# Rotary embedding on one core: VectorE's first product of its own row moved to the head of its own tile, and the last tile stored in one transfer

## The chip, the cores and the metric

One core of a Trainium2 chip runs the kernel. The metric is device time in microseconds (us), each kernel measured in repeated runs beside the kernel before on the same chip. "Span" is the time from the first to the last instruction of one profiled execution, some 1.8 us less than the device time of the same run.

## The reference, cut to what matters

```python
batch, seq, dim = (16, 512, 1024)          # float32, 16 heads of 64
x1, x2 = (x[..., :half_dim], x[..., half_dim:])
rotated = concatenate([x1 * cos - x2 * sin, x1 * sin + x2 * cos], axis=-1)
```

It reads 33.5 MB and writes 33.5 MB. Each output is two products and a sum: the element times its cosine, plus its partner in the other half of the head times plus or minus the sine.

## The kernel before: the parts that the change touches

The work goes in 8 tiles of 128 partitions and 8 rows (4 MB each), with room for five tiles at once. In each tile VectorE multiplies by the cosine into PSUM, GpSimd makes the sine products of rows 1 to 7, and VectorE adds two rows at a time (three pairs). Row 0, "its own row", has both products made by VectorE, and row 3 has its sine product from GpSimd. For these two rows TensorE adds the sine product to the cosine product in one PSUM accumulator, `own_ps`, and ScalarE copies the sum out. Row 0 and row 3 take turns in that accumulator.

```python
    def own_row(t):
        r0 = rows(t, ROW_OWN)
        own_product(t, r0)                 # in place, after cos_product has read r0
        ...                                # TensorE adds swapped(r0) to own_ps
        nc.scalar.copy(out=r0, in_=own_ps)

    cos_product(own_ps, 0, ROW_OWN)
    for t in range(NT):
        b1 = sin_rows(t, first[0], 2)
        if t > 0:
            own_row(t)
        p1 = pair_product(t, first[0])
        ...
        pair_sum(*p1, b1)
        p2 = pair_product(t, second[0])
        cos_product(own_ps, t, ROW_PE)     # row 3
        ...
        nc.scalar.copy(out=rows(t, ROW_PE), in_=own_ps)
        ...
        pair_sum(*p2, b2)
        p1 = pair_product(t, third[0])
        if t + 1 < NT:
            cos_product(own_ps, t + 1, ROW_OWN)
        pair_sum(*p1, b1)
        stores(t)                          # last tile: 4 rows, then 4 rows
```

All loads and stores of tiles are issued by SyncE.

## Time and profile before

| | before |
|---|---|
| device time, median of 6 runs | 163.12 us (163.02 to 163.49) |
| span of the profiled run | 161.1 us (its device time: 162.85) |
| busy: VectorE, GpSimd, TensorE, ScalarE | 85%, 79%, 40%, 11% |
| main DMA queue, share of sixteen engines | 97.4% |

How to read it: the prediction below shows the lines. A DMA share is a mean over sixteen engines. A stretch with share 1.00 has all of them at work. The packets of one transfer are dealt out to all sixteen. In short stretches a packet is counted where it starts, so in quarters of a microsecond a share can exceed 1, and 131 GB/s is one packet of 32 KB (131 GB/s x 0.25 us), 66 GB/s one of 16 KB, 82 GB/s one of 20 KB.

### The profile page before, as it was taken

Reading aid. Unit: us, or ns where it says so; the run is one execution under the profiler, and the core shown is the slowest. Engines: PE = TensorE matmul, PEld = TensorE weight load, DVE = VectorE, ACT = ScalarE, POOL = GpSimd, SP = SyncE. Lnnn points to the kernel's source line nnn. Section 1 sums busy time; section 2 is a strip of 40 time slices with the busy share of each in tenths; the row PEclk is TensorE's granted clock in tenths of the full one; section 3 lists DMA queues with packets and bytes.
Section 4 is the critical chain, followed back from the end, with each engine's and each line's share of the span. In section 5 each row is a group of like instructions: output and inputs, shape, how many; then the busy total and the mean of one; then the engine's idle time right before and its main releaser. Section 6 shows DMA issues by size and latency. Waiting matters only on the chain.

```text
span 161.1 us, 432 instructions
## 1 busy us (share of the span) xinstructions
PE 63.7 (40%) x72; PEld 20.4 (13%) x72; DVE 137.1 (85%) x77; ACT 18.5 (11%) x20; POOL 126.9 (79%) x38
## 2 busy tenths in 40 slices
PE   2363480535317170717144450808062622626000
PEld 0122020202011110202020200202020201111000
DVE  1159999999899999999899989999899989999400
ACT  3010201020202020020202020010102020202000
POOL 1195999999499999999999599972999999960000
PEclk9999959555855855595558555555955585557755
DMA  5999999799699699699999999698999999998994
GB/s 181 405 422 457 415 496 521 309 472 521 285 472 545 260 521 521 260 456 456 391 441 464 399 521 505 277 521 382 391 415 496 391 415 488 399 415 374 387 456 199
DMA packets 2257, 67.25 MB, mean 418 GB/s; under 512 B 272, under 2 KB 272, under 8 KB 336
## 3 DMA queue, kind: packets, MB, share of 16 engines
q1 hardware_dynamic: 2208, 67.18, 97.4%
q10 hardware_dynamic: 48, 0.07, 0.1%
q14 instruction: 1, 0.01, 0.0%
HBM read 33.69 MB, written 33.55 MB: 417 GB/s over the span
## 4 chain that ended last, share of the span: by engine, by line
DVE 46%; DMA 25%; PE 12%; issue 6%; ACT 3%; SPq 1%; DVEq 0%; ACTq 0%
DMA xt<-in_x_dram 25%; DVE xt L202 20%; DVE pd L153 18%; PE own_ps L187 12%; DVE xt L159 4%; DVE own_ps L153 4%; ACT xt L232 3%; SPq L78 1%; SPq L88 0%; DVEq L202 0%; ACTq L232 0%; DVEq L159 0%; DVEq L153 0%
## 5 line engine op out<-in xcount | busy, mean ns | idle before, releaser
L176 POOL TENSOR_TENSOR b<-xt,sns 128x2048 f32<-128x2048 f32 (+1 forms) x32 | 126.1, 3979 | 15.9 <-DMA xt<-in_x_dram 15.9
L202 DVE TENSOR_TENSOR xt<-pd,b 128x2048 f32<-128x2048 f32 x24 | 54.9, 2287 | 1.1 <-POOL b L176 0.2
L153 DVE TENSOR_TENSOR pd<-xt,cos_t 128x2048 f32<-128x2048 f32 x24 | 55.0, 2294 | 0.5
L187 PE MATMUL own_ps<-xt,ident 128*128 128x512 f32 x32 | 29.2, 1067 | 44.8 <-DVE xt L159 29.4
L187 PE MATMUL own_ps<-b,ident 128*128 128x512 f32 x32 | 29.3, 1072 | 33.3 <-DVE own_ps L153 30.9
L153 DVE TENSOR_TENSOR own_ps<-xt,cos_t 128x1024 f32<-128x1024 f32 x16 | 19.6, 1226 | 5.9 <-PE cos_t L123 2.8
L187 PEld LDWEIGHTS own_ps<-xt,ident 128*128 128x128 f32 x32 | 9.4, 324 | 64.5 <-issue 64.5
L187 PEld LDWEIGHTS own_ps<-b,ident 128*128 128x128 f32 x32 | 9.2, 316 | 52.9 <-issue 35.2
L194 ACT COPY xt<-own_ps 128x1024 f32<-128x1024 f32 x8 | 8.1, 1012 | 66.1 <-PE own_ps L187 66.1
L232 ACT COPY xt<-own_ps 128x1024 f32<-128x1024 f32 x8 | 8.1, 1012 | 54.8 <-PE own_ps L187 54.8
L159 DVE TENSOR_TENSOR xt<-xt,small 128x1024 f32<-128x1024 f32 x8 | 9.7, 1210 | 0.0
L124 DVE TENSOR_SCALAR sns<-small 128x256 f32<-128x256 f32 x1 | 0.4, 424 | 4.5 <-PE small L117 4.5
L117 PE MATMUL small<-sin_sb,spread 32*128 32x256 f32 x4 | 2.2, 661 | 2.7 <-DMA sin_sb<-in_sin_dram 2.7
L123 PE MATMUL cos_t<-cos_sb,spread 32*128 32x512 f32 x2 | 2.1, 1136 | 1.8 <-DMA cos_sb<-in_cos_dram 1.8
L117 PEld LDWEIGHTS small<-sin_sb,spread 32*128 32x128 f32 x4 | 1.2, 318 | 4.6 <-issue 4.6
L100 PE MATMUL own_ps<-zero 128*128 128x512 bf16 x2 | 1.0, 620 | 1.2 <-DVE zero L97 1.2
L125 ACT ACT_TABLE_LOAD x1 | 1.3, 1283 | 1.2 <-PEq L258 1.2
L97 DVE MEMSET zero<- 128x256 uint32 x1 | 0.3, 272 | 0.9 <-PEq L258 0.9
L125 ACT COPY sns<-small 128x256 f32<-128x256 f32 x1 | 0.4, 372 | 4.1 <-DVE sns L124 4.1
L128 ACT ACTIVATE sns<-small 128x256 f32<-128x256 f32 x1 | 0.4, 386 | 3.9 <-PE small L117 3.9
L120 DVE COPY small<-sns 128x64 f32<-128x64 f32 x2 | 0.4, 224 | 0.4 <-ACT sns L125 0.4
L123 PEld LDWEIGHTS cos_t<-cos_sb,spread 32*128 32x128 f32 x2 | 0.5, 308 | 2.5 <-DMA cos_sb<-in_cos_dram 2.5
(9 smaller groups left out, 1.6 us busy)
## 6 DMA issues: line engine op xcount, KB each, us to landing
out_dram<-xt SPq DMA_DIRECT2D x5, 4096.0 KB, 23.9
xt<-in_x_dram SPq DMA_DIRECT2D x3, 4096.0 KB, 21.4
out_dram<-xt SPq DMA_DIRECT2D x2, 2048.0 KB, 8.1
xt<-in_x_dram SPq DMA_DIRECT2D x1, 2560.0 KB, 12.1
xt<-in_x_dram SPq DMA_DIRECT2D x1, 1536.0 KB, 6.7
sin_sb<-in_sin_dram ACTq DMA_DIRECT2D x1, 64.0 KB, 4.0
cos_sb<-in_cos_dram SPq DMA_DIRECT2D x1, 64.0 KB, 6.7
xt<-in_x_dram SPq DMA_DIRECT2D x2, 34.8
```

Source lines behind the costliest of these rows:

```text
L78: nc.sync.dma_start(out=place, in_=x_v[at])
L100: nc.tensor.matmul(out=ps, lhsT=zero[:, :P], rhs=zero, start=True, stop=True)
L117: nc.tensor.matmul(out=sin_t, lhsT=spread, rhs=part, start=True, stop=True)
L123: nc.tensor.matmul(out=cos_t, lhsT=spread, rhs=cos_sb, start=True, stop=True)
L125: nc.scalar.copy(out=sns[:, :KK, 1, :], in_=sin_k)
L153: nc.vector.tensor_tensor(out=o, in0=i, in1=cb, op=ALU.mult)
L159: nc.vector.tensor_tensor(out=heads(r), in0=heads(r), in1=s, op=ALU.mult)
L176: nc.gpsimd.tensor_tensor(out=o, in0=i, in1=sb, op=ALU.mult)
L187: nc.tensor.matmul(out=ps, lhsT=ident, rhs=other, start=False, stop=True, skip_group_check=True)
L194: nc.scalar.copy(out=r0, in_=own_ps)
L202: nc.vector.tensor_tensor(out=r, in0=ps, in1=b, op=ALU.add)
L232: nc.scalar.copy(out=rows(t, ROW_PE), in_=own_ps)
```

## The change

Its intent: VectorE waited 0.5 us a tile for ScalarE to free the accumulator; with the last pair sum put ahead of the next tile's own-row product, the wait should be covered. And one store in place of two saves an issue and sends larger packets.

```diff
-        elif t == NT - 1:
-            store(t, 0, LAST_OUT)
-            store(t, LAST_OUT, KK)
         elif t > 1:
             store(t)
...
-    cos_product(own_ps, 0, ROW_OWN)
     for t in range(NT):
         first, second, third = PAIRS
         b1 = sin_rows(t, first[0], 2)
+        cos_product(own_ps, t, ROW_OWN)
         if t > 0:
             own_row(t)
...
         p1 = pair_product(t, third[0])
-        if t + 1 < NT:
-            cos_product(own_ps, t + 1, ROW_OWN)
         pair_sum(*p1, b1)
         stores(t)
```

More of the change, by code (lines that the diff above doesn't have):

```diff
@@ L23 @@
 FIRST = 3
-LAST_OUT = 4
 @with_exitstack
```

## The prediction

> **What bounds the kernel now.** I read the page's rows over time and its queue table first, then the stretches (windows), then VectorE's order of time, then SyncE's. From the page, the DMA row in 40 slices and the main queue:
>
> ```profile
> DMA  5999999799699699699999999698999999998994
> q1 hardware_dynamic: 2208, 67.18, 97.4%
> ```
>
> The main queue's packets fill 97.4% of sixteen engines' span, while VectorE has 85% and GpSimd 79%. The stretches show that this is a rate limit with one hole in it (columns: stretch, its length, busy time and count of PE, PEld, DVE, ACT, POOL, the granted clock, DMA share, GB/s):
>
> ```profile
> 2.00:148.00 146.00, 62.85 (x71) 20.24 (x70) 134.05 (x74) 17.10 (x20) 126.15 (x32) 0.65 1.00 431
> 148.00:149.50 1.50, 0.00 (x0) 0.00 (x0) 1.40 (x2) 0.56 (x1) 0.00 (x0) 1.00 0.29 120
> 149.50:159.20 9.70, 0.00 (x0) 0.00 (x0) 1.14 (x1) 0.00 (x0) 0.00 (x0) 0.56 0.98 416
> ```
>
> From 2 to 148 us the share is 1.00 at 431 GB/s: loads, then loads and stores, always queued. At 148 the queue runs dry: every earlier store has gone and the last tile isn't ready. Then the last tile's 4 MB take the final 9.7 us alone. SyncE's order of time shows what ends the hole:
>
> ```profile
> 134.59 0.33 SPq L82 DMA_DIRECT2D out_dram<-xt  x1
> 148.59 0.33 SPq L82 DMA_DIRECT2D out_dram<-xt  x1
> 150.67 0.33 SPq L82 DMA_DIRECT2D out_dram<-xt  x1
> ```
>
> The first is tile 6's whole store, the others the two halves of tile 7's. The first half goes at 148.59, as soon as ScalarE's copy of row 3 ends (147.55 + 1.01 = 148.56). It needs neither of the last VectorE sums. The second follows the last sum (148.35 + 2.29 = 150.64) and queues behind the first, so its time hides. The end of the span therefore hangs on the first byte of tile 7's store, plus 9.7 us of transfer, plus completion.
>
> The inferred chain puts 46% on VectorE, which is true of what delays that first byte, but not of the 146 us before. One VectorE period, tile 5's head to tile 6's head:
>
> ```profile
> 95.83 1.23 DVE L153 TENSOR_TENSOR own_ps<-xt,cos_t 128x1024 f32<-128x1024 f32 x1 [0.50 <-ACT xt L232]
> 96.96 2.29 DVE L202 TENSOR_TENSOR xt<-pd,b 128x2048 f32<-128x2048 f32 x1
> 99.16 1.21 DVE L159 TENSOR_TENSOR xt<-xt,small 128x1024 f32<-128x1024 f32 x1
> 100.29 2.29 DVE L153 TENSOR_TENSOR pd<-xt,cos_t 128x2048 f32<-128x2048 f32 x1
> 102.69 2.29 DVE L202 TENSOR_TENSOR xt<-pd,b 128x2048 f32<-128x2048 f32 x1
> 105.01 2.30 DVE L153 TENSOR_TENSOR pd<-xt,cos_t 128x2048 f32<-128x2048 f32 x1
> 107.22 1.22 DVE L153 TENSOR_TENSOR own_ps<-xt,cos_t 128x1024 f32<-128x1024 f32 x1
> 108.35 2.28 DVE L202 TENSOR_TENSOR xt<-pd,b 128x2048 f32<-128x2048 f32 x1
> 110.67 2.30 DVE L153 TENSOR_TENSOR pd<-xt,cos_t 128x2048 f32<-128x2048 f32 x1
> 113.47 1.23 DVE L153 TENSOR_TENSOR own_ps<-xt,cos_t 128x1024 f32<-128x1024 f32 x1 [0.50 <-ACT xt L232]
> ```
>
> The period is 113.47 - 95.83 = 17.64 us. The only wait in it is 0.50 us, the own-row product waiting for ScalarE to free the accumulator (own_ps). The reader should also take three kinds of start-to-start distance from these rows. An instruction after an independent one starts early: 1.13 after a one-row product, 2.20 to 2.21 after a two-row one. A product that reuses the accumulator just read by the sum in front of it starts 2.32 after. A sum straight after the product that it reads starts 2.40 after (100.29 to 102.69). So order alone costs up to 0.2 us a place.
>
> **What the Trainium skill says.** "DMA: Bandwidth & Descriptors", Specifications, gives a fabric ceiling of 435 GB/s and a first-byte latency of about 0.6 us for transfers issued from sync. The 431 GB/s above agree with the first, so faster compute can't shorten those 146 us; in quarter-microsecond stretches the burst after the issue at 148.59 appears at 149.25 to 149.50, so some 0.7 to 0.9 us here. "Perfetto Trace Analysis", DMA Optimizations, says that splitting a transfer may let some of it start sooner, where the DMA engines are idle; they are, at 148 to 149.5, and the first half is out 2.08 us before the second. "VectorE: DVE Perf Modes", The TRN2 errata, has (N+151)/0.96 ns for an fp32 tensor_tensor: 2291 ns for 2048 elements, where the rows have 2280 to 2300. The same page, The DRAIN you can't avoid, says a semaphore between neighbours costs nothing extra. These rows differ: 2.40 with the dependence against 2.21 without.
>
> **The change, part by part.**
>
> First part, the order on VectorE. No instruction is added or removed on any compute engine. In the new order the last sum follows its own product directly, and the own-row product is followed directly by the in-place product of the same row. That one overwrites what the own-row product has just read, and its semaphore is now one of a direct neighbour. A new period, from start to start:
> - own-row product to in-place product: 1.23 plus the gap of about 0.11 seen after a product written to PSUM (2.40 - 2.29) = 1.34. No row of before has this pair; 1.13 if it isn't held.
> - in-place product to first pair product 1.13; to its sum 2.40; to the second product 2.32; to the row-3 product 2.21; to the second sum 1.13; to the third product 2.32: together 11.51.
> - third product to the last sum 2.40 (2.21 + 0.59, the wait with its gap, before).
> - last sum to the next own-row product 2.20.
> Sum 17.45, against 17.64. The 0.5 us wait goes entirely: ScalarE's copy ends 2.8 us after the third product starts, and the own-row product now comes 4.6 after. But about 0.3 of it comes back as two dependences between neighbours, and 0.19 a period is left.
>
> Tile 0 to 1 had no wait (third product 23.00, own-row product 25.21), so there the new order only costs: the first pair product of tile 1 goes from 29.67 to about 30.07. From there one period brings tile 2's to 47.52 (47.38 before, after a 0.58 wait for its load, landed at 42.82, which the later place no longer meets). Five more periods: 47.52 + 5 x 17.45 = 134.77, against 135.57. Tile 7's remaining work is the same 15.07 us (135.57 to 150.64). VectorE ends at 149.84, 0.8 us earlier.
>
> Second part, one store. It waits for the last sum: issue at 149.84 + 0.03 = 149.87, in place of 148.59. The first byte comes 1.28 us later. Earlier stores are issued one or two microseconds sooner, but they join a queue that is full anyway, and the queue still runs dry at about 148. On the other side, the packets are of 32 KB and not 16 KB. An estimate from the rates above (9.7 us at 416 GB/s against 431 in the long stretch, where packets are of 32 KB and more) is at most 0.3 us; I take 0.13 off for it. One issue of 0.33 us less was hidden.
>
> Net: 0 over the streaming part, +1.28 - 0.13 = +1.15 at the end. The unprofiled time of 163.12 becomes about 164.2 (164.27, pulled down a little for a smaller neighbour gap).
>
> **Rivals.**
> - *The wait goes and the time with it.* Seven places of 0.5 us would be 3.5 us, some 159.6 us, faster by over 2%. For it: the chain has 46% VectorE and shows the ScalarE copy in it. Against: 431 GB/s for 146 us; VectorE's gain can only reach the hole at 148, which is about 1 us.
> - *The last store is hidden.* If VectorE got to the end by 148 or sooner, the queue would never dry and the kernel would gain that 1 us: about 162.2. That needs 0.45 us saved in each of six periods; the dependences take most of that.
> - *VectorE gains nothing.* If the neighbour gaps eat the whole 0.5 us, the store issues at 150.67, 2.08 us later: 163.12 + 2.08 - 0.13 = 165.1.
> - *No neighbour gap at the in-place product* (1.13, not 1.34). Seven places give 1.5 us back, VectorE ends at 148.4, the store issues 0.2 us before the first half did, and with the packets' 0.13 the time is 162.8.
> - *GpSimd becomes the bound.* Its products for a tile take 3 x 4.52 + 2.35 = 15.9 us, under 17.45, and they end at 143.4. Its waits are for loads, which don't move. I give it little.
>
> **Range and chances.** 164.2 us, with 163.3 to 164.9 eight times in ten: the low end is most of the way to the unheld in-place product, the high end near the rival without gain. The three timed runs of before lie within 0.36 us. Two per cent is 3.26 us either way. Nothing above reaches 166.4; 159.9 needs the transfer limit to be wrong. Faster 0.01, within 2% 0.97, slower 0.02.
>
> **What would show it.** In the changed profile: no ScalarE wait ahead of the own-row product; last sums 2.40 after their product; in-place products 1.34 after the own-row product; a period of 17.45; DMA share 1.00 until about 148, then a hole longer by a good microsecond; a single issue near 149.9; some 9.6 us of transfer after it. I am wrong if the hole is gone, if the streaming part itself gets faster or slower than 431 GB/s, or if the in-place pair has another distance, which moves the end by 0.07 us for each 0.01.

## The result, and the profile after

The changed kernel took 163.44 us (median of 6 runs, 163.18 to 163.76) against 163.12. The ratio is 1.0015, with a 95% interval of 0.9999 to 1.0031. A ratio here is the mean time of one kernel's fast runs over that of the other's of the same rounds, so it isn't quite the ratio of the medians. It is 0.24 us of 163.2, where 1.1 was forecast. The time lies in the predicted range, but the difference is less than a quarter of the one forecast, and not clear of noise.

The page's DMA row and main queue, the stretches, and SyncE's last issue (same columns as in the prediction):

```profile
DMA  5999999699699799799999999898999999996996
q1 hardware_dynamic: 2064, 67.18, 97.0%
```

```profile
2.00:148.00 146.00, 63.73 (x71) 20.41 (x70) 135.49 (x75) 17.66 (x20) 126.17 (x32) 0.68 1.00 430
148.00:149.50 1.50, 0.00 (x0) 0.00 (x0) 1.50 (x1) 0.00 (x0) 0.00 (x0) 1.00 0.11 44
149.50:159.20 9.70, 0.00 (x0) 0.00 (x0) 0.30 (x1) 0.00 (x0) 0.00 (x0) 0.51 0.88 378
```

```profile
149.87 0.33 SPq L81 DMA_DIRECT2D out_dram<-xt  x1
```

The streaming part is as it was (1.00, 430 GB/s), the hole is longer, and the single store issues at 149.87 us, which is the predicted figure. VectorE's order of time, one period from tile 5's head to tile 6's:

```profile
97.59 1.22 DVE L152 TENSOR_TENSOR own_ps<-xt,cos_t 128x1024 f32<-128x1024 f32 x1
98.84 1.22 DVE L158 TENSOR_TENSOR xt<-xt,small 128x1024 f32<-128x1024 f32 x1
99.98 2.29 DVE L152 TENSOR_TENSOR pd<-xt,cos_t 128x2048 f32<-128x2048 f32 x1
...
110.36 2.29 DVE L152 TENSOR_TENSOR pd<-xt,cos_t 128x2048 f32<-128x2048 f32 x1
112.75 2.29 DVE L201 TENSOR_TENSOR xt<-pd,b 128x2048 f32<-128x2048 f32 x1
114.96 1.22 DVE L152 TENSOR_TENSOR own_ps<-xt,cos_t 128x1024 f32<-128x1024 f32 x1
...
147.50 2.29 DVE L201 TENSOR_TENSOR xt<-pd,b 128x2048 f32<-128x2048 f32 x1
```

From tile 1 on no wait is left. (One of 0.40 us for ScalarE stands in tile 0, at 19.90; the first profile of before has none there, the second has the same.) The period is 114.96 - 97.59 = 17.37 us (17.64 before, 17.45 predicted). The in-place product comes 1.25 after the own-row product, the last sum 2.39 after its product. So VectorE did what was forecast; it ended at 149.79 us, forecast 149.84. What was wrong comes after that.

The end in quarters of a microsecond shows it. Before:

```profile
148.75:149.00 0.25, 0.00 (x0) 0.00 (x0) 0.25 (x1) 0.00 (x0) 0.00 (x0) 1.00 0.31 131
149.00:149.25 0.25, 0.00 (x0) 0.00 (x0) 0.25 (x1) 0.00 (x0) 0.00 (x0) 1.00 0.00 0
149.25:149.50 0.25, 0.00 (x0) 0.00 (x0) 0.25 (x1) 0.00 (x0) 0.00 (x0) 1.00 1.38 590
...
158.50:158.75 0.25, 0.00 (x0) 0.00 (x0) 0.00 (x0) 0.00 (x0) 0.00 (x0) 0.50 2.16 918
158.75:159.00 0.25, 0.00 (x0) 0.00 (x0) 0.00 (x0) 0.00 (x0) 0.00 (x0) 0.50 0.31 131
159.00:159.25 0.25, 0.00 (x0) 0.00 (x0) 0.00 (x0) 0.00 (x0) 0.00 (x0) 0.50 0.15 66
```

After:

```profile
148.75:149.00 0.25, 0.00 (x0) 0.00 (x0) 0.25 (x1) 0.00 (x0) 0.00 (x0) 1.00 0.31 131
149.00:149.25 0.25, 0.00 (x0) 0.00 (x0) 0.25 (x1) 0.00 (x0) 0.00 (x0) 1.00 0.01 0
...
159.00:159.25 0.25, 0.00 (x0) 0.00 (x0) 0.00 (x0) 0.00 (x0) 0.00 (x0) 0.50 1.22 524
159.25:159.50 0.25, 0.00 (x0) 0.00 (x0) 0.00 (x0) 0.00 (x0) 0.00 (x0) 0.50 3.66 1573
```

In both, a single 32 KB packet of tile 6 starts as late as 148.75 to 149.00 us. At 1.21 us for such a packet, the engine that carries it is busy until about 150.1. In before, the other fifteen begin tile 7 from 149.25 on, and that one engine only when it is done; at the end it is alone with the last 16 KB packet (66 GB/s in 159.00 to 159.25). It had no hole, and it set the end. In the changed kernel all engines are idle when the store's first bytes come (150.70 in the packet records; the late engine is done at 150.10). They start together and finish together: the last packets of four start at 159.00 to 159.25 and those of twelve at 159.25 to 159.50, with no straggler.

The packet records (every packet's start, length, queue and size, kept with each trace) give the sizes, counted here from the span's start. They carry no engine number; the ends of the sixteen engines are those of the last sixteen packets that close the store. The fifteenth ends at 159.43 before and at 160.60 after: 1.17 us later, where 1.15 was predicted. But the end of before is the sixteenth engine's, at 159.86, and that of after is at 160.61, so the end moved by 0.75 only (the spans by 0.72). The first profile of before is also a run on the fast side, 162.85 us for a median of 163.12. A second pair of profiles, told below, has a smaller step still.

### The profile page after: what moved, and what is told of

It reads as the page before. It is cut to its first block, busy times and chain, and to the rows that moved or that the text cites. A ratio compares the mean times of both kernels' runs of the same rounds, so it can differ in the third digit from the quotient of the medians.

```text
span 161.8 us, 432 instructions
## 1 busy us (share of the span) xinstructions
PE 64.5 (40%) x72; PEld 20.5 (13%) x72; DVE 137.8 (85%) x77; ACT 18.5 (11%) x20; POOL 126.9 (78%) x38
## 4 chain that ended last, share of the span: by engine, by line
DVE 35%; DMA 33%; POOL 13%; issue 9%; PE 2%; ACT 1%; DVEq 0%; POOLq 0%; SPq 0%
DMA xt<-in_x_dram 17%; DMA out_dram<-xt 17%; DVE pd L152 15%; DVE xt L201 14%; POOL b L175 13%; DVE own_ps L152 2%; PE own_ps L186 2%; DVE xt L158 2%; ACT xt L193 1%; DVE small L119 0%; DVEq L201 0%; POOLq L175 0%; SPq L77 0%; SPq L81 0%
## 5 line engine op out<-in xcount | busy, mean ns | idle before, releaser
L186 PE MATMUL own_ps<-xt,ident 128*128 128x512 f32 x32 | 29.7, 1081 | 42.7 <-DVE xt L158 22.2
```

What stands on the lines that cost most here:

```text
L186: nc.tensor.matmul(out=ps, lhsT=ident, rhs=other, start=False, stop=True, skip_group_check=True)
```

## The experiments

Two theories were put to the chip. **A**: one DMA engine runs about a packet behind the others and sets the end; the hole is free until that engine is done. **B**, the prediction's: each microsecond by which the first byte comes later counts in full. "3+5" and "4+4" are the rows in the last tile's two stores.

| run | order | last store | issue of tile 7's first byte | median us | ratio to before | 95% | fifteen engines end, the last ends |
|---|---|---|---|---|---|---|---|
| before_again | old | 4+4 | 148.75 | 163.24 | 1.0002 | 0.9977 to 1.0027 | 159.57, 160.34 |
| after_again | new | one | 149.56 | 163.44 | 1.0017 | 0.9994 to 1.0040 | 160.29, 160.46 |
| store_only | old | one | 150.83 | 164.55 | 1.0086 | 1.0065 to 1.0108 | 161.55, 161.58 |
| order_only | new | 4+4 | 147.64 | 163.26 | 1.0014 | 0.9995 to 1.0033 | 159.04, 160.14 |
| split3 | old | 3+5 | about 140.9 | 163.17 | 1.0013 | 0.9992 to 1.0034 | 158.87, 160.07 |
| order_split3 | new | 3+5 | about 139.7 | 163.03 | 1.0005 | 0.9984 to 1.0026 | 159.02, 160.56 |
| after_cos_first | new | one | 149.14 | 163.42 | 1.0030 | 1.0004 to 1.0055 | 159.88, 160.66 |
| after_late | new | one | 152.10 | 165.65 | 1.0163 | 1.0137 to 1.0189 | 162.81, 162.84 |

(The two "about" figures come from rows in which the view merges two issues: the row's end less one issue of 0.33 us. The last column is from the packet records of the profiled run; the first profiles have 159.43, 159.86 before and 160.60, 160.61 after. The runs were made in several sessions, each beside the kernel before on its own chip; issues and ends are those of one profiled run, the ratios those of four to six runs.)

The last column shows A at a glance. Where the hole is closed (order_only, split3, order_split3), fifteen engines end some 0.4 to 0.7 us earlier than in the two profiles of before, and the last ends at 160.07 to 160.56, where those two have 159.86 and 160.34.

### store_only: the second part alone

```diff
-        elif t == NT - 1:
-            store(t, 0, LAST_OUT)
-            store(t, LAST_OUT, KK)
```

> The order of before, with the last tile's store in one transfer: the second part of the change alone. The store must wait for the last sum, so it should issue near 150.7 us where the first half issued at 148.6 before, and all sixteen DMA engines stand idle for about 2 us. Theory A (one DMA engine runs about one packet behind the others, is still busy with tile 6 when the first half issues, and sets the end of before; for the other fifteen the hole is free up to about half a microsecond): 2.08 us later first byte, less 0.44 us that the laggard had cost at the end, less 0.1 us for larger packets: +1.3 to +1.5 us, about 164.5 us. Theory B (the prediction: every microsecond of later first byte counts in full): +1.95 us, about 165.1 us.

Measured 164.55 us, +1.40 by the ratio. SyncE's order of time has the issue at 150.83, 2.24 us later than before:

```profile
150.83 0.33 SPq L82 DMA_DIRECT2D out_dram<-xt  x1
```

A's figure, not B's: the interval is 1.06 to 1.76, and B has 1.95. Some 0.8 us of the delay was free, what larger packets save included.

### order_only: the first part alone

```diff
+LAST_OUT = 4
...
+        elif t == NT - 1:
+            store(t, 0, LAST_OUT)
+            store(t, LAST_OUT, KK)          # the rest as in the changed kernel
```

> The new order on VectorE, with the last tile's store still in two halves: the first part of the change alone. The first half should issue 0.7 us earlier than before (near 147.8). Theory A (one DMA engine behind the others sets the end): the first byte for fifteen engines comes earlier, the laggard's does not, the time is that of before within 0.2 us, about 163.1. Theory B (the hole counts in full): the hole of about 0.85 us nearly closes, about 162.4 us.

```profile
147.64 0.33 SPq L82 DMA_DIRECT2D out_dram<-xt  x1
```

```profile
148.00:149.50 1.50, 0.00 (x0) 0.00 (x0) 1.50 (x1) 0.00 (x0) 0.00 (x0) 1.00 0.77 328
```

Measured 163.26 us. The first half issued at 147.64, 0.95 us earlier than before, the share in the hole's stretch rose from 0.29 to 0.77, and the time didn't fall. A holds.

### split3: the hole taken away in the old order

```diff
-LAST_OUT = 4
+LAST_OUT = 3
```

> The order of before, the last tile stored as 3 rows and 5 rows and not 4 and 4: the first transfer waits for the first pair sum and the own row only, so it issues near 140.3 us, long before the queue is dry, and the second, at 150.7, lands behind it. The hole at 148 to 149.5 us must be gone from the profile in either theory. Theory A: the laggard engine never idled in before, so the time is that of before within 0.2 us: 163.1. Theory B: 0.85 us to 1.2 us faster: about 162.1.

Measured 163.17 us. The stretch that held the hole (0.43 in before) and the end:

```profile
148.50:149.50 1.00, 0.00 (x0) 0.00 (x0) 0.90 (x2) 0.52 (x1) 0.00 (x0) 0.50 0.92 389
```

```profile
158.00:158.25 0.25, 0.00 (x0) 0.00 (x0) 0.00 (x0) 0.00 (x0) 0.00 (x0) 0.50 0.57 246
158.25:158.50 0.25, 0.00 (x0) 0.00 (x0) 0.00 (x0) 0.00 (x0) 0.00 (x0) 0.50 0.02 0
158.50:158.75 0.25, 0.00 (x0) 0.00 (x0) 0.00 (x0) 0.00 (x0) 0.00 (x0) 0.50 0.20 82
158.75:159.00 0.25, 0.00 (x0) 0.00 (x0) 0.00 (x0) 0.00 (x0) 0.00 (x0) 0.50 0.01 0
159.00:159.25 0.25, 0.00 (x0) 0.00 (x0) 0.00 (x0) 0.00 (x0) 0.00 (x0) 0.50 0.00 0
159.25:159.50 0.25, 0.00 (x0) 0.00 (x0) 0.00 (x0) 0.00 (x0) 0.00 (x0) 0.50 0.19 82
```

The hole is gone, and nothing is won. The last full round starts by 158.25, and after that single 20 KB packets (82 GB/s) follow one another, 0.76 us each, the last of them starting over a microsecond after the others' last. This is the plainest picture of a mean that hides one engine.

### order_split3: both at once, the candidate for a better version

The new order with the two stores of order_only, and:

```diff
-LAST_OUT = 4
+LAST_OUT = 3
```

> New order and 3 rows plus 5 rows: both parts that could remove the hole together, the candidate for a version better than both. Theory A: the floor is the slowest DMA engine's share of the bytes, 163.0 to 163.2 us, no better than before. Theory B: 162.1 us or less.

Measured 163.03 us, ratio 1.0005: the same as before. No arrangement of these two parts beats the kernel before.

### after_late: what a microsecond of VectorE is worth after the change

```diff
         p1 = pair_product(t, third[0])
+        if t == NT - 1:
+            cos_product(p1[0], t, third[0], 2)
```

> The changed kernel with the last pair product of the last tile done twice (result unchanged), so that VectorE ends about 2.3 us later: what a microsecond of VectorE is worth there. Both theories: all sixteen DMA engines already stand idle when the single store issues, so it counts in full, +2.2 to +2.4 us, 165.7 us. A smaller step would mean that something other than the last sum releases the last store.

Measured 165.65 us, +2.66 over before by the ratio, so 2.2 to 2.4 more than the changed kernel, as both theories had it. The issue came at 152.10:

```profile
152.10 0.33 SPq L81 DMA_DIRECT2D out_dram<-xt  x1
```

With store_only this gives the relation: 1.27 us later (150.83 to 152.10) costs 1.26 us by the ratios, give or take half a microsecond (their intervals), and 1.26 by the two spans: the full price. Going back from store_only at that price, the cost is zero at 150.83 - 1.40 = 149.43 us, with some 0.35 us either way. So the hole is free up to about there, 0.84 us after before's issue at 148.59. The changed kernel's own two profiles, 149.87 for +0.24 and 149.56 for +0.28, would put it at 149.63 and 149.28.

### before_again and after_again: the scatter

Both kernels unchanged, with a second profile each.

> The kernel before, a second time and with a second profile, to size the scatter between runs of one kernel: ratio 1.000 within 0.002, and in the profile one late engine again, a single 32 KB packet still starting after 148.5 us and the store's first half issued at 148.6.

> The changed kernel, a second time and with a second profile, beside the kernel before on the same chip: 1.0015 to 1.004 of it, that is 163.4 to 163.8 us. In the profile VectorE without a wait, the single store at 149.5 to 150.1, all sixteen engines idle ahead of it, and no late engine at the end. Theory B of the prediction would have it at 164.2 or more.

Ratios of 1.0002 and 1.0017: the small step holds, and stays within noise. In the second profile of before the first half issued at 148.75 and the late engine ended 0.77 us after the rest in the packet records:

```profile
158.75:159.00 0.25, 0.00 (x0) 0.00 (x0) 0.00 (x0) 0.00 (x0) 0.00 (x0) 0.50 2.32 983
...
159.50:159.75 0.25, 0.00 (x0) 0.00 (x0) 0.00 (x0) 0.00 (x0) 0.00 (x0) 0.50 0.17 66
```

Both spans are 161.6 us here. One expectation was a little off: in after_again a 32 KB packet still starts at 149.50 to 149.75, beside the issue at 149.56, so its late engine had no hole (it was busy to 150.78, the others' first bytes came at 150.39), and in the packet records it still ends 0.17 us after the rest. How far that engine lags differs from run to run.

### after_cos_first: an earlier VectorE in the changed kernel

```diff
-    load(0, 0, FIRST)
     nc.sync.dma_start(out=cos_sb, in_=cos_v)
+    load(0, 0, FIRST)
```

> The changed kernel with the cosine table's load issued ahead of the first rows' and not behind it, so VectorE's first product can start 1 to 3 us earlier than at 10.4 us. In the changed kernel VectorE runs from there to the end without meeting a load, so its end and the single store should come as much earlier, by 148.5 us or sooner. Theory A (slowest DMA engine is the floor): the store then meets the queue before or as the late engine runs dry, and the time falls to the floor of 163.0 to 163.2, not below. Theory B (hole counts in full): 162.4 or less.

Measured 163.42 us, above A's 163.0 to 163.2: a miss in size. VectorE's first product did start 2.9 us earlier (7.52), but 2.1 of that went into a wait at 20.44 for GpSimd, which itself had waited for the rest of tile 0, and the store issued at 149.14. B's 162.4 didn't come. In the profile a single 32 KB packet starts at 159.25 to 159.50: the late engine ends 0.79 us after the rest. The edit also had a side effect: the table's packets now go first, so the first rows' packets start at 2.23 us and not at 1.75, and the middle one of the sixteen engines ends tile 6 at 149.1, where the changed kernel's two profiles have 148.9 and 148.8. So some 0.2 to 0.3 us of the miss can be the whole stream shifted later. The six times spread over 162.89 to 164.18.

### Why is one engine late? nofetch_split3, morefetch_split3, fewer_dve_split3, min_dve_split3

The page of before lists one packet of an instruction queue:

```profile
q1 hardware_dynamic: 2208, 67.18, 97.4%
q10 hardware_dynamic: 48, 0.07, 0.1%
q14 instruction: 1, 0.01, 0.0%
```

In the packet records this is 8 KB in mid-run. It took 0.31 us, and a 32 KB packet that starts as it ends took 1.78 us where the others took 1.21. One engine has lost some 0.9 us there. (Theory **F**: this makes the late engine. **S**: something else does.) The Trainium skill, "DMA: Bandwidth & Descriptors", Queues, rings and completion order, says that row 14 of the queues is the runtime's own, for refills among others, and that each engine takes turns between the rows that have work; the trace agrees in the queue's number and name, but for one packet of morefetch_split3 below, which has queue 8. Four kernels, all from split3, which has no hole to hide in:

nofetch_split3 leaves out TensorE's additions for row 0 (wrong result):

```diff
-        for ps, r in zip(parts(own_ps), parts(r0)):
-            pe_add(ps, swapped(r))
```

> The kernel of the 3+5 rows experiment with TensorE's additions of the own row left out (wrong result in one row of eight, on purpose): 32 of its 72 matmuls and their weight loads fewer, everything that moves data as it was. It asks why one DMA engine is about a microsecond behind. Theory F (an 8 KB fetch of instructions, the one packet of the instruction queue on the page, held up one of the sixteen DMA engines in mid-run at 82 us; it took 0.31 us and stretched the packet beside it from 1.21 to 1.78 us): if TensorE's instructions were those fetched, the queue is gone from the page, the last single packets at 158.75 to 159.50 us are gone, and the time falls by 0.6 to 0.9 us, to about 162.4. Theory S (an engine that is slow for another reason): no change, 163.1 within 0.2. If the instruction packet stays on the page, it belonged to another engine and the run decides nothing.

162.77 us, ratio 0.9988 (0.9968 to 1.0009), and the packet stayed on the page. By its own terms it decides nothing, except that the packet isn't owed to those TensorE instructions. Its time lies between the two theories.

Its packet records do decide something. A packet starts within some 10 ns of the end of the one before it on the same engine, so one engine can be followed from packet to packet as long as no other engine ends a packet at the same moment. Here the last packet of all (158.80 to 159.56) leads back, over 61 packets and never with a second candidate, to the 1.78 us packet that starts at 83.54, as the instruction packet ends. So the engine that the instruction packet held up is the late one. In split3 and before_again the same walk ends at two candidates, of which the held-up packet is one.

morefetch_split3 adds instructions:

```diff
+    for _ in range(64):
+        nc.tensor.matmul(out=small[:, 384:392], lhsT=zero[:, :P], rhs=zero[:, :8], start=True, stop=True)
```

> The kernel of the 3+5 rows experiment with 64 tiny matmuls of zeros into an unused corner added to TensorE's idle time at the start (result unchanged): 128 more instructions, so one or two more instruction packets on the page. Theory F: if the same DMA engine serves them it falls behind by another 0.6 to 0.9 us each and the time rises to 163.8 or more; if another engine serves them, the time stays, with a second engine as late as the first. Theory S: no change, 163.1 within 0.2, and no second late engine.

163.88 us, ratio 1.0048 (1.0024 to 1.0073), against split3's 1.0013. The page has two more packets of instruction queues; by the packet records the second of queue 14 is one of 40 bytes at the start, which order_split3 and after_late have too, so the one that counts is queue 8's, of 16 KB:

```profile
q8 instruction: 1, 0.02, 0.0%
q14 instruction: 2, 0.01, 0.0%
```

The direction is F's. The 16 KB packet came at 105.14 us and took 1.02 us, and the 64 KB packet that starts as it ends took 2.92 us where the others took 2.42. At the end two engines are late, at 159.78 and 160.81, the rest by 159.11. That fits one late engine for each packet: walked back, the later one meets the packet held up by the 16 KB (one of three candidates) and the earlier one that held up by the 8 KB (one of eight, so weaker). That the 16 KB packet holds the added instructions isn't shown.

fewer_dve_split3 leaves out VectorE's three one-row products of each tile (wrong result):

```diff
-    cos_product(own_ps, 0, ROW_OWN)
...
-        own_product(t, r0)
...
-        cos_product(own_ps, t, ROW_PE)
...
-        if t + 1 < NT:
-            cos_product(own_ps, t + 1, ROW_OWN)
```

> The kernel of the 3+5 rows experiment with VectorE's three one-row products of every tile left out (wrong result in two rows of eight, on purpose): 24 VectorE instructions fewer, every load and store as it was, and VectorE far off the end. Two questions. First, whether VectorE sets anything once the hole is closed: theory A says no, so the time must stay at or above 162.2 us although VectorE ends many microseconds earlier; theory B's VectorE-bound reading would give 155 us or less. Second, whether the instruction packet in mid-run was VectorE's: if it is gone from the page and theory F holds, the late engine's 0.9 us is gone too and the time is 162.2 to 162.6; if it is gone and the time stays at 163.1, the late engine has another cause; if it stays on the page, this is left open.

163.40 us, ratio 1.0009 (0.9983 to 1.0035). VectorE ended at 146.5 us in place of 150.9, with no gain, so it sets nothing once the queue is kept full. The packet stayed, but the records have it some 17 us later than in split3 (100.72 against 83.53). It follows VectorE's progress through its instructions: in every run that has this packet, VectorE has 63 or 64 instruction records by the time it starts, here too.

min_dve_split3 also leaves out two of the three pair products and sums of each tile (wrong result):

```diff
-        p1 = pair_product(t, first[0])
...
-        pair_sum(*p1, b1)
-        p2 = pair_product(t, second[0])
...
-        pair_sum(*p2, b2)
```

> The 3+5 rows kernel with nearly all of VectorE's work left out (no one-row products, and one pair product and sum a tile in place of three: wrong result on purpose), every load and store as it was. The run before it moved the instruction packet from 82 to 100 us by leaving out 24 VectorE instructions, so the packet seems to be VectorE's; with another 32 fewer it should be gone from the page. Theory F (that packet delays one DMA engine by 0.9 us and that engine sets the end): packet gone, no 82 GB/s single packets a microsecond after the rest at the end, 162.2 to 162.6 us. Theory S (the late engine has another cause): packet gone and the time still 163.1 within 0.2, with single late packets at the end. In both, VectorE's absence by itself must not make the kernel faster than 162.2, because the queue is full from 2 us on.

162.16 us, ratio 0.9943 (0.9926 to 0.9960): 0.93 us faster. The queues, all of them, and the end:

```profile
q1 hardware_dynamic: 2208, 67.18, 98.0%
q10 hardware_dynamic: 48, 0.07, 0.1%
```

```profile
158.00:158.25 0.25, 0.00 (x0) 0.00 (x0) 0.00 (x0) 0.00 (x0) 0.00 (x0) 0.50 0.38 164
158.25:158.50 0.25, 0.00 (x0) 0.00 (x0) 0.00 (x0) 0.00 (x0) 0.00 (x0) 0.50 0.01 0
158.50:158.75 0.25, 0.00 (x0) 0.00 (x0) 0.00 (x0) 0.00 (x0) 0.00 (x0) 0.50 0.02 0
```

The instruction packet is gone (VectorE has 41 instruction records in all, so it never gets to the 63rd), the late packets are gone, and so is the microsecond, all together. Less VectorE work by itself isn't the cause. fewer_dve_split3 had VectorE 4 us ahead, the packet still there, and no gain. And in the packet records fifteen engines end at 158.79 here and at 158.87 in split3, while the last ends at 158.82 here and at 160.07 there: all that went is the late engine. So theory F stands. What isn't tried is a kernel with a right result and few enough VectorE instructions to need no such packet.

## Why the prediction was right or wrong

- *What bounds the kernel: the transfer rate from 2 to 148 us.* Right. It is 430 GB/s after the change too, and taking VectorE's end from 150.9 to 146.5 us in fewer_dve_split3 won nothing.
- *The wait goes, dependences between neighbours take back part.* Right. The period is 17.37 against 17.45; the in-place product 1.25 after its neighbour against 1.34 (no row of before had that pair, and it wasn't the unheld 1.13 either).
- *VectorE ends at 149.84, store issued at 149.87.* Right: 149.79 and 149.87. VectorE's first product was 0.41 us later in that run (10.41, 10.00 before) and nothing absorbs such a shift any more; the smaller gap paid it back. That the two cancel is luck: the second profile had 10.10, an end at 149.48 and an issue at 149.56. (Another in-place distance was one of the prediction's signs of being wrong. It came, but it isn't what failed.)
- *Larger packets save about 0.13.* Right in size. The records have 0.11 on fifteen engines: first byte 1.28 later (149.42 to 150.70), end 1.17 later.
- *The first byte comes 1.28 us later, and that counts in full: net +1.15.* This is the step that failed. It was right for fifteen engines (1.17) and wrong for the end. In before the end was the sixteenth engine's, which was still carrying tile 6 when the first half was issued. The prediction took all sixteen engines to be idle at 148 to 149.5, where splitting a store could pay; one was not. The true term is the delay beyond about 149.43 us (store_only's figure), not beyond 148.59: some 0.8 us of it are free. That leaves 149.87 - 149.43 = 0.44 us, or 0.13 us for the second profile's 149.56, and 0.24 to 0.28 were measured.
- *Rivals.* The rival "the last store is hidden" said that a hole that closed would win 1 us. order_only, split3 and order_split3 closed it and won nothing, for the same reason. The rival that all waits turn into time is refuted by the same runs.

The lines that could have told me were in the profile of before: one 32 KB packet starting at 148.75 in the middle of the "idle" stretch, and one 16 KB packet alone at the end. I read the mean share of a 1.5 us stretch and took it for the state of each engine. The Trainium skill, "Perfetto Trace Analysis", What "DMA-bound" means, names "Specific DMA engines" as the first of the things a kernel can be bound on; this case agrees, with 0.44 and 0.77 us between the last engine and the rest in before, and 1.20 in split3.

## What to carry to other kernels

A gap in the mean DMA share is worth only what the latest engine loses in it: look for single packets inside the gap and after the last full round before putting a price on it. Where transfers stream at their limit, as here at 430 GB/s from 2 to 148 us, a faster engine can win only at the two ends, and a split last store kept the first byte off the critical path here: joining the two halves in the old order cost 1.40 us, and the smaller packets of the halves only some 0.1. When an order is changed to cover a wait, count the dependences that become neighbours; here they took back about half of what the wait had cost.

## What the Trainium skill lacked or had wrong

- "DMA: Bandwidth & Descriptors", Queues, rings and completion order: it names the runtime's queue row and its refills; what one costs the transfers on the same DMA engine in mid-run, no page has. Here one 8 KB instruction packet took 0.31 us, its neighbour 1.78 in place of 1.21 us, and the kernel without it and with most of VectorE's instructions gone was 0.93 us faster by the ratio (medians 162.16 against 163.18 us).
- "Perfetto Trace Analysis", What "DMA-bound" means: it has the single engine, but no figure for how far one can lag. Here the last engine ended 0.44 and 0.77 us after the rest in the two profiles of before, and the mean share was 0.29 over 1.5 us while that engine had no idle time.
- "VectorE: DVE Perf Modes", The DRAIN you can't avoid: from eight tensor_copy instructions the section has it that a semaphore after each costs nothing extra. Here a dependence between neighbours does cost: a sum straight after its product starts 2.40 us after it, an independent instruction 2.21; for the in-place one-row product it is 1.25 against 1.13. The section also says that an instruction that isn't held starts earlier; it has no figure for it.
